# Two layers of a hybrid mixer network on one core: attention stacks fetched a head ahead, two or three merge blocks put ahead of the first scores, and layer 1's middle modulations made in layer 0's ConvFFN

## The chip, the core and the metric

The kernel runs on one core of a Trainium2 chip. The metric is the device time of one execution in microseconds (us). Before the change the median of three runs is 2433.31 us, the lowest 2432.21 and the highest 2433.33. TensorE (PE) multiplies matrices, VectorE (DVE) and ScalarE (ACT) work on tiles in on-chip memory, POOL (GpSimd) here does little but issue transfers, and SP (SyncE) issues the loads of weights. TensorE takes its instructions in the order in which they stand in the program, as each of the engines does.

## What is computed

512 latent tokens and 256 context tokens of width 1024 go through two layers. Each layer normalises the tokens, scales and shifts them with modulations made from a conditioning vector (adaLN), feeds four mixers and their gates from one input projection, merges the four with gates, projects, adds, normalises again, and runs a gated feed-forward network with a short convolution (ConvFFN, 2816 wide). One of the four mixers is differential attention with four heads of two score maps each:

```python
def _diff_softmax(q, k, v, lam):
    s = jnp.einsum('bhcqd,bhckd->bhcqk', q, k).astype(F32) * (DA_HEAD ** -0.5)
    p = jax.nn.softmax(s, axis=-1)
    w = p[:, :, 0] - lam * p[:, :, 1]
    return jnp.einsum('bhqk,bhkv->bhqv', w.astype(v.dtype), v)

def _adaln(cond, w, b, n_chunks):
    m = jax.nn.silu(cond) @ w[:, :n_chunks * D_MODEL] + b[:n_chunks * D_MODEL]
    return [t[:, None, :] for t in jnp.split(m, n_chunks, axis=-1)]
```

Latent tokens read context and latent tokens (768 keys), context tokens read only context (256 keys). In the second layer the context gives only its keys, values and states; its outputs aren't needed, so layer 1 has 512 query tokens and layer 0 has 768. Queries and keys are normalised per head and rotated before the scores.

## The kernel before

Activations lie channel-major: a tile has 128 channels as partitions and up to 768 tokens as columns. All large products are made in high and low parts: `load_split` loads a weight block (`load_raw`, L179, three buffers, SP's queue), casts its high part on ScalarE (L191) and subtracts on VectorE for the low part (L192); `proj` (L204) makes three matmuls for each pair of blocks (L218), 512 or 256 columns wide.

Modulations (`ada`, L258): 24 pairs of blocks for each layer, named by `PAIRS`. A pair is two loads of 512 KB, sixteen small matmuls (L280), a copy and a closing (L267). `FIRST` holds pairs 0 to 7 (shift and scale of the first norm), `REST` pairs 8 to 19 (the gate of the mixers, shift and scale of the second norm), `LAST` pairs 20 to 23 (the gate of the ConvFFN). Layer l's `REST` runs between the blocks of its own merges; `LAST` and the next layer's `FIRST` run in its ConvFFN, one step after each of its 22 blocks.

Attention (`da_mix`, L882): for each pair of heads `da_prep` (L843) normalises and rotates q and k, splits them into high and low parts and spills them to DRAM (`dstk00q` is layer 0, pair 0, q), on POOL's queue (L861). `da_stack` (L865) loads them back for one head, stacked so that high and low parts meet in one product: four loads for q (L874, tile `dstq`) and two for k (L877, tile `dstk`). Both take tiles from a pool with tag z, which has eight buffers; the values `dv` hold two of them for the whole attention. Then, for each block of 128 queries, `scores` makes four matmuls (two for context queries) into one PSUM tile `ps_s` of three banks, of which there is one buffer (L920 to L927), reduces it to the negated maximum on VectorE (`d_nm`, L929) and takes two exponentials on ScalarE (L933). `values` handles two query blocks: it weighs on VectorE (L940 to L943), transposes on TensorE (`ps_wt`, L949), copies to `dwT` (tag h, six buffers) on ScalarE, and multiplies with the values (`ps_o`, L964). It is called three query blocks behind the scores (`DA_AHEAD`). The stack of a head is asked for when the head begins.

Merges: `merge_branch` (L1208) goes over eight blocks of output channels; for each it makes a gate (`gate`, L1203, 24 or 48 matmuls `ps_g`, a tanh), then the product of the branch (`ps_p`), and two VectorE operations. In layer 1 the six gates of the last branch are made early, into buffers of tag h.

The order on the engines is set by a scheduler, which takes instructions by priority and by its estimate of when they are ready: mixers are written with a high priority (`MIXER_FIRST`), so that merge blocks and modulations, written behind the mixer, fill what it leaves on TensorE. `tc.issue_after(x)` holds an instruction back until x stands in the order.

Of the kernel before, what the change touches and what calls it, by code (L numbers as in the profile page):

```python
# [8 lines left out]
F32 = mybir.dt.float32  # L9
# [8 lines left out]
P = 128  # L18
D = 1024
KT = 8  # L20
# [17 lines left out]
DA_AHEAD = 3  # L38
EARLY = 6
# [15 lines left out]
# pairs of ada blocks (chunk * KT + k): shift1 and scale1, gate1, shift2 and scale2, gate2  # L55
# [23 lines left out]
def backbone(ctx, tc, xT, cT, w_ada, w_in, w_v, w_ga, w_branch, w_out, w_up, w_down, vec,  # L79
# [6 lines left out]
    gp_ = ctx.enter_context(tc.tile_pool(name="gp", bufs=25))  # L86
# [10 lines left out]
    def Z(name, shape=None, dt=F32):  # L97
        return gp_.tile(shape or [P, T], dt, tag="z", name=name, bufs=8)
# [57 lines left out]
    # recurrence gates: half biases and LRU_C / 2 times the log-sigmoid of the decay  # L156
# [20 lines left out]
    last = [None]  # L177

    def load_raw(src, nk=KT, cols=P, tag="wraw"):  # L179
        t = wp.tile([P, nk, cols], F32, tag=tag, name="wraw", bufs=3)  # L180
        last[0] = nc.sync.dma_start(t, src).ins
        return t
# [21 lines left out]
    def proj(name, w, act, sg, use, c0=0, cut=None, late=False):  # L204
        """use(ps, a, b) takes the product for the tokens a..b; a cut splits the products, not what use gets;
        late: the low parts of the activations come last"""
        whi, wlo = w
        n = len(act)
        for (a, b) in sg:
            ps = PF(name)  # L210
            step = cut or b - a
            for c in range(a, b, step):
# [4 lines left out]
                for i, (k, wt, x_) in enumerate(terms):  # L217
                    nc.tensor.matmul(ps[:, c - a:d - a], wt[:, k, c0:c0 + P], act[k][x_][:, c:d],  # L218
                                     start=i == 0, stop=i == 3 * n - 1)
            use(ps[:, 0:b - a], a, b)  # L220

    def proj_all(name, loads, act, parts, use, tail=2):
        """the blocks m of a product; use(m, ps, a, b); the last ones go part by part"""
# [10 lines left out]
    def proj_tok(l, which, h, name):  # L234
        """token-major values: tiles of three token blocks"""
# [20 lines left out]
    mods = [cpool.tile([P, 48, 2], F32, name=f"mod{l}") for l in range(DEPTH)]  # L256

    def ada(l, pairs, first=False):  # L258
        """pair p makes the blocks PAIRS[p] of the modulations"""
# [46 lines left out]
    def norm_mod(l, x, g, sh, sc, parts, marks=(None, None)):  # L306
        """the parts are normalised one after the other"""
# [68 lines left out]
    # rstd over partition groups of size n (block-ones matrix bo)  # L376
# [12 lines left out]
    # accurate exp on a small tile  # L389
# [38 lines left out]
    def s5_prep(l):  # L428
# [40 lines left out]
        # unit phasor of 8 steps  # L469
# [5 lines left out]
        # input gains k = (lb - 1) / lam  # L475
# [18 lines left out]
        # phasor tables  # L494
# [25 lines left out]
        for hf in range(2):  # L520
            kps = []
            for d in range(2):
# [16 lines left out]
                # C * lam^k, k = 0..8 (reversed order for the backward direction)  # L539
# [43 lines left out]
                # Bb * lam^k: k = 7 - s (forward), s (backward)  # L583
# [259 lines left out]
    def da_prep(l, i, qk, sg, qgs, rp):  # L843
        """normalised, rotated q and k of heads 2i, 2i+1, parked as exact high and low parts"""
# [38 lines left out]
    def da_mix(l, qks, vt_, lat_only):  # L883
# [25 lines left out]
        stks = [da_prep(l, i, qks[i], sg, qgs, rp) for i in range(2)]  # L909
        o = None  # L910

# [25 lines left out]
        def weights(hd, qt, k0, l2, ps_):  # L937
            """the weights of a head, transposed"""
# [17 lines left out]
        def values(pr):  # L956
            """two blocks of queries of a head, side by side in the array"""
# [22 lines left out]
        for hd in range(4):  # L980
            st = da_stack(stks[hd // 2], hd % 2, sg)
            for qt in range(e // P):
                pend.append(scores(hd, qt, *st))
# [191 lines left out]

    def chain(*gens):
        for g in gens:
            yield from g
# [7 lines left out]
    def weave(main, fill, n=1, flush=True):  # L1186
        """Emit the steps of main with n steps of fill after each of them; returns main's value."""
# [20 lines left out]
    def merge_branch(l, b, h, y, acc, sg, first, gates=()):  # L1208
        """gates: those of the first blocks, where they are there already"""
# [279 lines left out]
```

## Time and profile before

| | us |
|---|---|
| median of three runs | 2433.31 |
| span of the profiled execution | 2429.0 |
| TensorE busy | 2290.4 (94%) |
| VectorE busy | 1322.8 (54%) |
| ScalarE busy | 917.3 (38%) |
| POOL busy | 101.6 (4%) |

The profiled execution lies 4.3 us below the median, which also counts what lies around the span. Below, stretches of the program are named by their time in this span: layer 0's attention stage is 438.8 to 693, its last merges and its ConvFFN 693 to 1446, layer 1's attention stage 1728 to 1967. In a row of a timeline the bracket is the idle time of the engine just before the instruction, and what ended it. PEclk is the granted clock of TensorE as a share of its upper level, 2.4 GHz; 0.50 is the lower level, 1.2 GHz.

### The profile page before, as it was taken

What the parts mean: (1) busy time and instruction counts of PE and PEld (TensorE: products, weight loads), DVE (VectorE), ACT (ScalarE), POOL (GpSimd) and SP (SyncE); (2) the same over time, 40 slices, a digit from 0 to 9 for tenths busy, and PEclk for the clock granted to TensorE, in tenths of its full rate; (3) what the DMA queues carried; (4) which work ended last, traced back from release to release, by engine and by line L of the source; (5) the groups of instructions that cost most, each with busy time, mean ns of one, the idle gap of its engine ahead of it and who ended that gap; (6) DMA issues with size and microseconds to landing.
All of it is one profiled execution on the core that took longest, in us unless ns stands there. A gap on an engine that the chain in (4) does not pass through costs nothing.

```text
span 2429.0 us, 34598 instructions
## 1 busy us (share of the span) xinstructions
PE 2290.4 (94%) x13848; PEld 1906.5 (78%) x13848; DVE 1322.8 (54%) x2831; ACT 917.3 (38%) x1430; POOL 101.6 (4%) x164
## 2 busy tenths in 40 slices
PE   6999999688899999999999999999877899999999
PEld 4788788576788878888888887878655689888887
DVE  7786564565584495343334366557454556444443
ACT  6734134334442243122221247522533454323322
POOL 0010000100000010000000000000110000000000
PEclk9999989889999999999999989999988899999999
DMA  7243243533223233222222232244445324332332
GB/s 259 81 138 121 81 127 107 128 96 87 76 96 117 72 123 122 74 96 63 94 76 81 80 121 72 77 144 156 123 117 127 91 88 130 130 104 87 95 106 86
DMA packets 128176, 258.04 MB, mean 106 GB/s; under 512 B 52816, under 2 KB 61072, under 8 KB 128016
## 3 DMA queue, kind: packets, MB, share of 16 engines
q1 hardware_dynamic: 85136, 222.13, 28.8%
q0 software_dynamic: 42880, 33.70, 5.7%
q8 instruction: 109, 1.79, 0.3%
q14 instruction: 51, 0.42, 0.1%
HBM read 230.78 MB, written 24.87 MB: 105 GB/s over the span
## 4 chain that ended last, share of the span: by engine, by line
PE 67%; issue 22%; DMA 5%; DVE 2%; ACT 2%; POOL 1%; SPq 0%; POOLq 0%; ACTq 0%; DVEq 0%
PE ps_fd L218 13%; PE ps_fa L218 11%; PE ps_fg L218 11%; PE ps_g L218 9%; PE ps_p L218 2%; PE ps_wo L218 2%; PE ps_vdv L244 1%; PE ps_vgv L244 1%; PE ps_u L218 1%; PE ps_lx L218 1%; PE ps_gg L218 1%; PE ps_ada L280 1%; PE ps_ly L218 1%; DMA wraw<-in_w_in_dram 1%; PE ps_go L1138 1%
## 5 line engine op out<-in xcount | busy, mean ns | idle before, releaser
L191 ACT CAST whi<-wraw 128x1024 fp32r<-128x1024 f32 (+2 forms) x284 | 280.6, 989 | 645.0 <-PE ps_fd L218 209.5
L192 DVE TENSOR_TENSOR wlo<-wraw,whi 128x1024 fp32r<-128x1024 f32 (+2 forms) x284 | 325.6, 1147 | 306.5 <-ACT whi L191 282.7
L218 PE MATMUL ps_g<-hi,whi 128*128 128x512 f32 (+1 forms) x768 | 283.7, 369 | 5.2 <-ACT gate L1205 4.5
L218 PE MATMUL ps_g<-lo,whi 128*128 128x512 f32 (+1 forms) x768 | 279.8, 364 | 0.0
L218 PE MATMUL ps_g<-hi,wlo 128*128 128x512 f32 (+1 forms) x768 | 279.6, 364 | 0.0
L218 PE MATMUL ps_fg<-hi,whi 128*128 128x512 f32 (+1 forms) x544 | 194.0, 358 | 3.2 <-ACT hi L364 3.1
L218 PE MATMUL ps_fg<-hi,wlo 128*128 128x512 f32 (+1 forms) x544 | 190.9, 352 | 0.0
L218 PE MATMUL ps_fa<-hi,whi 128*128 128x512 f32 (+1 forms) x528 | 188.1, 356 | 0.0
L218 PE MATMUL ps_fa<-hi,wlo 128*128 128x512 f32 (+1 forms) x528 | 187.3, 355 | 0.0
L218 PE MATMUL ps_fa<-lo,whi 128*128 128x512 f32 (+1 forms) x528 | 187.0, 354 | 0.0
L218 PE MATMUL ps_fd<-ulo,whi 128*128 128x512 f32 (+1 forms) x528 | 186.8, 354 | 0.0
L218 PE MATMUL ps_fd<-uhi,whi 128*128 128x512 f32 (+1 forms) x528 | 186.3, 355 | 0.1
L218 PE MATMUL ps_fg<-lo,whi 128*128 128x512 f32 (+1 forms) x544 | 186.1, 351 | 0.0
L218 PE MATMUL ps_fd<-uhi,wlo 128*128 128x512 f32 (+1 forms) x528 | 186.0, 354 | 0.0
L218 PEld LDWEIGHTS ps_g<-hi,whi 128*128 128x128 f32 x768 | 148.6, 194 | 35.8 <-ACT gate L1205 7.0
L218 PEld LDWEIGHTS ps_g<-hi,wlo 128*128 128x128 f32 x768 | 148.6, 193 | 23.4 <-issue 2.7
L218 PEld LDWEIGHTS ps_g<-lo,whi 128*128 128x128 f32 x768 | 148.7, 194 | 22.7 <-issue 2.7
L1274 DVE SCALAR_TENSOR_TENSOR x<-ps_fd,mod,x 128x512 f32<-128x512 f32 (+1 forms) x96 | 62.9, 660 | 161.6 <-PE ps_fd L218 161.6
L218 PEld LDWEIGHTS ps_fg<-hi,whi 128*128 128x128 f32 x544 | 104.5, 192 | 23.5 <-ACT hi L364 5.3
L929 DVE TENSOR_REDUCE d_nm<-ps_s 128x2 f32<-128x1536 f32 (+1 forms) x40 | 61.6, 1541 | 105.8 <-PE ps_s L923 101.0
L218 PEld LDWEIGHTS ps_fg<-hi,wlo 128*128 128x128 f32 x544 | 104.9, 193 | 13.6
L1267 DVE TENSOR_TENSOR fy<-ps_fa,fy 128x512 f32<-128x512 f32 x66 | 39.8, 602 | 137.7 <-PE ps_fa L218 136.2
(471 smaller groups left out, 4812.7 us busy)
## 6 DMA issues: line engine op xcount, KB each, us to landing
wraw<-in_w_ada_dram SPq DMA_DIRECT2D x96, 512.0 KB, 4.5
wraw<-in_w_in_dram SPq DMA_DIRECT2D x92, 512.0 KB, 3.5
wraw<-in_w_up_dram SPq DMA_DIRECT2D x88, 512.0 KB, 3.4
wraw<-in_w_down_dram SPq DMA_DIRECT2D x32, 384.0 KB, 3.2
wraw<-in_w_down_dram SPq DMA_DIRECT2D x32, 320.0 KB, 3.0
wraw<-in_w_branch_dram SPq DMA_DIRECT2D x16, 512.0 KB, 3.5
wraw<-in_w_out_dram SPq DMA_DIRECT2D x16, 512.0 KB, 3.7
x<-in_xT_dram SPq DMA_DIRECT2D x16, 384.0 KB, 4.4
```

The source lines that it names most:

```text
L191: nc.scalar.copy(hi, raw)
L192: nc.vector.tensor_sub(lo, raw, f32(hi))
L218: nc.tensor.matmul(ps[:, c - a:d - a], wt[:, k, c0:c0 + P], act[k][x_][:, c:d], start=i == 0, stop=i == 3 * n - 1)
L244: nc.tensor.matmul(ps[:, 0:256], a[:, tt * P:(tt + 1) * P], wt[:, k % 4, :], start=st, stop=sp_)
L280: mi = nc.tensor.matmul(ps[32 * g:32 * g + 32, 0:2 * P], cs[:, 4 * j + g, :], raw[:, g, :], start=j == 0, stop=j == 1, tile_position=(0, 3 ...
L929: v.tensor_reduce(nm, sv, AX.X, ALU.max, negate=True)
L1138: nc.tensor.matmul(po[:, oc:oc + 64], sb_[d][:, cc, 2 * pr_:2 * pr_ + 2, :].rearrange("p h v -> p (h v)"), dirs[d][0][:, c * 64:c * 64 + 6 ...
L1267: proj("ps_fa", wa, h, sg, lambda ps, a, b: v.tensor_mul(y[:, a:b], ps, y[:, a:b]), late=f < LATE2)
L1274: v.scalar_tensor_tensor(x[m][:, a:b], ps, mods[l][:, 5 * KT + m, i:i + 1], x[m][:, a:b], op0=ALU.mult, op1=ALU.add)
```

## The change

The stack of head `hd + 1` is asked for when head `hd` begins, and that of head 0 before the second pair of heads is prepared. Tag z has ten buffers instead of eight, so that two stacks fit beside `dv`. The first two steps of `da_mix` are written ahead of the merges; then two (layer 0) or three (layer 1) blocks of branch 3's merge are written, and the first scores are held back until the last matmul of these stands in the order. Layer 1's `REST` moves into layer 0's ConvFFN, behind layer 1's `FIRST`, and each block of a ConvFFN is now followed by two steps instead of one. Raw weights get a fourth buffer. To pay for the buffers, the on-chip area for the descriptors of POOL's transfers falls from its default of 16384 bytes a partition to 4096.

```diff
+DA_LEAD = (2, 3)
...
-    gp_ = ctx.enter_context(tc.tile_pool(name="gp", bufs=25))
+    gp_ = ctx.enter_context(tc.tile_pool(name="gp", bufs=27))
...
     def Z(name, shape=None, dt=F32):
-        return gp_.tile(shape or [P, T], dt, tag="z", name=name, bufs=8)
+        return gp_.tile(shape or [P, T], dt, tag="z", name=name, bufs=10)
...
     def load_raw(src, nk=KT, cols=P, tag="wraw"):
-        t = wp.tile([P, nk, cols], F32, tag=tag, name="wraw", bufs=3)
+        t = wp.tile([P, nk, cols], F32, tag=tag, name="wraw", bufs=4 if tag == "wraw" else 3)
...
-                    nc.tensor.matmul(ps[:, c - a:d - a], wt[:, k, c0:c0 + P], act[k][x_][:, c:d],
-                                     start=i == 0, stop=i == 3 * n - 1)
+                    lastp[0] = nc.tensor.matmul(ps[:, c - a:d - a], wt[:, k, c0:c0 + P], act[k][x_][:, c:d],
+                                                start=i == 0, stop=i == 3 * n - 1).ins
...
-        stks = [da_prep(l, i, qks[i], sg, qgs, rp) for i in range(2)]
+        stks = [da_prep(l, 0, qks[0], sg, qgs, rp)]
+        st = da_stack(stks[0], 0, sg)
+        stks.append(da_prep(l, 1, qks[1], sg, qgs, rp))
         o = None
+        lead = yield
...
         for hd in range(4):
-            st = da_stack(stks[hd // 2], hd % 2, sg)
+            cur = st
+            if hd < 3:
+                st = da_stack(stks[(hd + 1) // 2], (hd + 1) % 2, sg)
             for qt in range(e // P):
-                pend.append(scores(hd, qt, *st))
+                with tc.issue_after(lead) if hd == 0 and qt == 0 else nullcontext():
+                    pend.append(scores(hd, qt, *cur))
...
+    def sent(gen, value):
+        try:
+            gen.send(value)
+            while True:
+                yield
+                next(gen)
+        except StopIteration as s:
+            return s.value
...
-        rest = ada(l, REST)
+        rest = ada(l, REST) if l == 0 else iter(())
         acc = []
-        if l > 0:
-            for _ in range(FILL1):
-                next(rest)
...
-        yd_ = mixer(da_mix(l, (qk0, qk1), dv, lat_only))
-        drain(zipgen(merge_branch(l, 3, h, yg, acc, sg, False), rest, 1))
+        dm = da_mix(l, (qk0, qk1), dv, lat_only)
+        with first():
+            next(dm)
+            next(dm)
+        mb = merge_branch(l, 3, h, yg, acc, sg, False)
+        for _ in range(DA_LEAD[l]):
+            next(mb)
+            next(rest, None)
+        yd_ = mixer(sent(dm, lastp[0]))
+        drain(zipgen(mb, rest, 1))
...
-        nxt = chain(ada(l, LAST), *([ada(l + 1, FIRST)] if l + 1 < DEPTH else []))
+        nxt = chain(ada(l, LAST), *([ada(l + 1, FIRST), ada(l + 1, REST)] if l + 1 < DEPTH else []))
...
-        ffn(l, h, x, sg, lambda: next(nxt, None))
+        def side():
+            for _ in range(2):
+                next(nxt, None)
+        ffn(l, h, x, sg, side)
...
-    nc = _bacc.Bacc("TRN2", target_bir_lowering=False, num_devices=1)
+    nc = _bacc.Bacc("TRN2", target_bir_lowering=False, num_devices=1, dynamic_dma_scratch_size=4096)
```

Three places of the engines' orders follow; the lines of the changed kernel are some two to eight higher for the same statement. First POOL in layer 0's attention, from the k loads of head 0 on, before the change (`dstq<-dstk00q` and `dstk<-dstk00k` load the heads of pair 0, `01` those of pair 1; the rows with `dhi` and `dlo` are the spills of pair 1):

```order
L877 DMA dstk<-dstk00k 128x1x768 x2
L861 DMA dstk01q<-dhi 4x32x768
L861 DMA dstk01q<-dlo 4x32x768
L874 DMA dstq<-dstk00q 64x1x768 x2
L861 DMA dstk01k<-dhi 4x32x768
L861 DMA dstk01k<-dlo 4x32x768
L874 DMA dstq<-dstk00q 64x1x768 x2
L877 DMA dstk<-dstk00k 128x1x768 x2
L874 DMA dstq<-dstk01q 64x1x768 x4
L877 DMA dstk<-dstk01k 128x1x768 x2
```

and after it:

```order
L879 DMA dstk<-dstk00k 128x1x768 x2
L876 DMA dstq<-dstk00q 64x1x768 x4
L863 DMA dstk01q<-dhi 4x32x768
L863 DMA dstk01q<-dlo 4x32x768
L879 DMA dstk<-dstk00k 128x1x768
L863 DMA dstk01k<-dhi 4x32x768
L863 DMA dstk01k<-dlo 4x32x768
L879 DMA dstk<-dstk00k 128x1x768
L876 DMA dstq<-dstk01q 64x1x768 x4
L879 DMA dstk<-dstk01k 128x1x768 x2
```

Head 1's four q loads stood behind both q spills of pair 1 and around its k spills, and now follow head 0's k loads as one piece; its k loads are now on either side of the k spills.

Then TensorE in layer 1 around the first scores of head 0 (L920 to L923 before, L925 to L928 after; `ps_g` and `ps_p` are matmuls of merge blocks, `ps_ada` those of modulations), before the change:

```order
L218 MATMUL ps_p<-ylo,whi 128x512
L218 MATMUL ps_p<-yhi,wlo 128x512
L280 MATMUL ps_ada<-wraw,cs 32x256 x6
L920 MATMUL ps_s<-dstk,dstq 128x512
L921 MATMUL ps_s<-dstk,dstq 128x256
L280 MATMUL ps_ada<-wraw,cs 32x256 x2
L922 MATMUL ps_s<-dstk,dstq 128x256
L923 MATMUL ps_s<-dstk,dstq 128x512
L218 MATMUL ps_g<-hi,whi 128x512
L218 MATMUL ps_g<-lo,whi 128x512
```

and after it:

```order
L220 MATMUL ps_g<-hi,whi 128x512
L220 MATMUL ps_g<-lo,whi 128x512
L220 MATMUL ps_g<-hi,wlo 128x512
L220 MATMUL ps_g<-hi,whi 128x512
L925 MATMUL ps_s<-dstk,dstq 128x512
L926 MATMUL ps_s<-dstk,dstq 128x256
L220 MATMUL ps_g<-lo,whi 128x512
L220 MATMUL ps_g<-hi,wlo 128x512
L220 MATMUL ps_g<-hi,whi 128x512
L927 MATMUL ps_s<-dstk,dstq 128x256
L928 MATMUL ps_s<-dstk,dstq 128x512
L220 MATMUL ps_g<-lo,whi 128x512
```

The pairs of modulations between the scores are gone, and gate matmuls of the third merge block stand there. Between the squares of q (`dqss`) and these scores 96 matmuls of 512 columns of merge blocks stood before, and 132 stand now.

Last, TensorE at the last scores of layer 1's attention (`ps_wt` are the transposes of the weights, `ps_o` the products with the values), before the change:

```order
L218 MATMUL ps_g<-hi,wlo 128x512
L218 MATMUL ps_g<-hi,whi 128x512
L920 MATMUL ps_s<-dstk,dstq 128x512
L921 MATMUL ps_s<-dstk,dstq 128x256
L922 MATMUL ps_s<-dstk,dstq 128x256
L923 MATMUL ps_s<-dstk,dstq 128x512
L964 MATMUL ps_o<-dwT,dv_14997 64x128 x6
L964 MATMUL ps_o<-dwT,dv_14998 64x128 x6
L949 MATMUL ps_wt<-cst,dp 128x128 x4
L218 MATMUL ps_g<-lo,whi 128x512
L218 MATMUL ps_g<-hi,wlo 128x512
```

and after it:

```order
L954 MATMUL ps_wt<-cst,dp 128x128 x6
L925 MATMUL ps_s<-dstk,dstq 128x512
L926 MATMUL ps_s<-dstk,dstq 128x256
L927 MATMUL ps_s<-dstk,dstq 128x256
L928 MATMUL ps_s<-dstk,dstq 128x512
L954 MATMUL ps_wt<-cst,dp 128x128 x6
L925 MATMUL ps_s<-dstk,dstq 128x512
L926 MATMUL ps_s<-dstk,dstq 128x256
L927 MATMUL ps_s<-dstk,dstq 128x256
L928 MATMUL ps_s<-dstk,dstq 128x512
L969 MATMUL ps_o<-dwT,dv_15126 64x128 x6
L969 MATMUL ps_o<-dwT,dv_15127 64x128 x6
```

Before, gate matmuls stand ahead of the last scores and behind the transposes; now, from the fourth query block of head 2 to the end of head 3, only transposes and products with the values stand between the scores, and the gate matmuls follow behind the last of these.

## Rows read from the trace of the kernel before

**Rows 1.** Windows by stage: us, TensorE busy (records), PEclk, DMA share, GB/s
```profile
438.80:693.00 254.20, 206.25 (x1333) 0.89 0.36 94
693.00:1446.00 753.00, 745.12 (x4472) 0.99 0.29 94
...
1728.00:1967.00 239.00, 194.71 (x1027) 0.87 0.44 114
...
sum 2429.00, PE 2290.38; mean PE 381.73
```

**Rows 2.** Timeline of TensorE at each head's first scores: start, us, instruction, idle before
```profile
456.73 0.77 PE L920 MATMUL ps_s<-dstk,dstq 128*128 128x512 f32 x1 [17.88 <-issue]
...
525.11 0.77 PE L920 MATMUL ps_s<-dstk,dstq 128*128 128x512 f32 x1 [7.28 <-DMA dstk<-dstk00k]
...
581.89 0.76 PE L920 MATMUL ps_s<-dstk,dstq 128*128 128x512 f32 x1 [9.54 <-DMA dstk<-dstk01k]
...
637.19 0.76 PE L920 MATMUL ps_s<-dstk,dstq 128*128 128x512 f32 x1 [8.31 <-DMA dstk<-dstk01k]
...
1772.90 0.77 PE L920 MATMUL ps_s<-dstk,dstq 128*128 128x512 f32 x1 [14.93 <-issue]
...
1835.53 0.77 PE L920 MATMUL ps_s<-dstk,dstq 128*128 128x512 f32 x1 [8.87 <-DMA dstk<-dstk10k]
...
1878.63 0.77 PE L920 MATMUL ps_s<-dstk,dstq 128*128 128x512 f32 x1 [6.34 <-DMA dstk<-dstk11k]
...
1922.24 0.76 PE L920 MATMUL ps_s<-dstk,dstq 128*128 128x512 f32 x1 [6.18 <-issue]
```

**Rows 3.** Windows of TensorE behind the six later waits, the last one and the sum
```profile
1918.97:1932.62 13.65, 9.46 (x30) 0.50 0.14 37
sum 61.44, PE 36.19; mean PE 6.03
```

**Rows 4.** Timeline of POOL at requests of head 1, layer 0, and of layer 1
```profile
509.53 1.57 POOL L877 DMA_DIRECT2D dstk<-dstk00k  x2 [36.56 <-PE ps_ada L267]
...
1731.14 0.75 POOL L861 DMA_DIRECT2D dstk10q<-dhi  x1 [25.39 <-ACT dhi L197]
...
1864.17 1.57 POOL L877 DMA_DIRECT2D dstk<-dstk11k  x2 [43.14 <-PE ps_s L923]
```

**Rows 5.** DMA queues and issues from 509 to 526 us: packets, MB, share; KB, us to landing
```profile
q0 software_dynamic: 4192, 1.59, 57.9%
...
dstk<-dstk00k POOLq DMA_DIRECT2D x2, 384.0 KB, 15.2
```

**Rows 6.** Window from the squares of q to layer 1's first scores, columns as in Rows 1
```profile
1723.80:1773.00 49.20, 30.89 (x140) 0.82 0.60 145
```

**Rows 7.** Timeline of TensorE in that window: a modulation pair, first and last of 27 matmuls
```profile
1733.21 1.07 PE L280 MATMUL ps_ada<-wraw,cs 128*32 128x256 f32 x16
...
1736.06 0.39 PE L218 MATMUL ps_g<-hi,wlo 128*128 128x512 f32 x1
...
1741.98 0.39 PE L218 MATMUL ps_p<-ylo,whi 128*128 128x512 f32 x1
```

**Rows 8.** Groups by line and shape, 1770 to 1965: count, busy us, mean ns, idle before
```profile
L933 ACT ACTIVATE dp<-ps_s,d_nm 128x768 f32<-128x768 f32 x32 | 28.6, 901 | 9.6 <-DVE d_nm L929 8.9 <-ACT dwT L951 0.7
L929 DVE TENSOR_REDUCE d_nm<-ps_s 128x2 f32<-128x1536 f32 x16 | 28.1, 1754 | 36.6 <-PE ps_s L923 36.6
...
L949 PE MATMUL ps_wt<-cst,dp 128*128 128x128 f32 x96 | 17.2, 300 | 0.6 <-ACT dwT L951 0.6
L943 DVE SCALAR_TENSOR_TENSOR dp<-dp,d_rl 128x768 f32<-128x768 f32 x16 | 16.3, 1018 | 0.5
...
L964 PE MATMUL ps_o<-dwT,dv 128*64 128x128 f32 x187 | 14.6, 284 | 0.1
```

**Rows 9.** DMA issues of the whole run: count, KB each, median us to landing
```profile
wraw<-in_w_ada_dram SPq DMA_DIRECT2D x96, 512.0 KB, 4.5
...
dstk00k<-dhi POOLq DMA_DIRECT2D x1, 384.0 KB, 8.9
```

More of the change, by code (lines that the diff above doesn't have):

```diff
@@ L177, in backbone @@
     last = [None]
+    lastp = [None]
     def load_raw(src, nk=KT, cols=P, tag="wraw"):
-        t = wp.tile([P, nk, cols], F32, tag=tag, name="wraw", bufs=3)
+        t = wp.tile([P, nk, cols], F32, tag=tag, name="wraw", bufs=4 if tag == "wraw" else 3)
         last[0] = nc.sync.dma_start(t, src).ins
```

## The prediction

> **What bounds the kernel now.** I read the busy time of TensorE stage by stage first [rows 1]. Over the whole it is busy for 2290.38 us of a span of 2429.00, so no other engine can be the bound, and the change can win only time that TensorE does not use. The span lies 4.3 us below the median of the runs, 2433.31; the sum is made on the span and carried over to the median.
>
> From 693 to 1446 us (layer 0's last merges and its ConvFFN) TensorE is idle for 7.9 us in 753. In the two attention stages it is idle for 48.0 us in 254.2 (layer 0) and 44.3 us in 239 (layer 1), and the granted clock averages 0.89 and 0.87 there. These two are the stages to look at.
>
> Next, TensorE's timeline at the first scores of each head (L920); the bracket is the idle time before [rows 2]. Layer 0 waits 17.88 us for head 0, then 7.28, 9.54 and 8.31 for heads 1 to 3. Layer 1 waits 14.93 for head 0, then 8.87, 6.34 and 6.18. Of the six later waits five end with the DMA of a k stack (`dstk`); the sixth is put down to "issue", and stands at the same place of the same loop. The six sum to 25.13 + 21.39 = 46.5 us.
>
> Each wait also takes the clock. In the six stretches right behind them, one of which is shown, the granted clock is 0.50, the lower level (1.2 GHz), and TensorE is busy in them for 36.19 us [rows 3]. At the upper level the same work takes half, so the price is 18.1 us. The six head changes together cost 46.5 + 18.1 = **64.6 us**.
>
> Why a stack is late: POOL's requests stand until TensorE's last work on an earlier head releases buffers. In layer 0 head 1's k stack is asked for at 509.53, after 36.56 us of standing; in layer 1 head 2's at 1864.17, after 43.14 us, released by `ps_s` [rows 4]. The scores of these heads begin 15.6 and 14.5 us later [rows 2]. In the first of these stretches a head's loads put 4192 packets into the software queue, and a k load takes 15.2 us to land [rows 5].
>
> The Trainium skill, page "DMA: Bandwidth & Descriptors", section "Anatomy of one DMA — SWDGE (gpsimd) path", gives a fit of 2.0 us plus bytes over 436e3 per us, which makes an estimate of 2.9 us for such a load. The rows say 15.2, and the measurement decides. By the page the loads would have some 3 us to hide at a head change, and the gain would be nearer 15 than 65.
>
> **The change part by part.** *Stacks a head ahead.* With ten tiles instead of eight the next head's loads are asked for while the present head runs. In POOL's order head 1's four q loads now follow head 0's k loads directly, and head 2's loads wait for head 0's last scores, not head 1's. From one head's first scores to the next are 43 to 68 us [rows 2], and a stack takes about 15 [rows 5]: it lands at least 25 us before it is wanted, and all six waits go, 64.6 us. What is late next is the softmax chain of the head itself. As a lower bound some waits shrink to 2 or 3 us and keep a piece of their low clock: 50 us.
>
> *Merge blocks ahead of the first scores.* In layer 0 TensorE's order up to the first scores is the same before and after, so the 17.88 us stay. In layer 1 the way from the squares of q (1723.8) to the first scores takes 49.2 us, of which TensorE is busy for 30.89 [rows 6]; about 2.6 of these are lost to a low clock (0.82 on average), so there are 28.2 us of work and 21 lost. The way is one of spills and loads, on POOL from 1731.14 on [rows 4], and stays as it is. After the change 132 matmuls of 512 columns stand on it. From 1736.06 to 1741.98 26 such follow each other [rows 7], 0.228 us each: 30.1 us, and 2.2 us of small ones, 32.3. Lost: 49.2 - 32.3 = 16.9 instead of 21, a gain of **4 us** (0 if the way grows, 9 if it shortens).
>
> *What these blocks no longer cover.* They are missing at the end of layer 1's attention. Before, up to 19 gate matmuls stand between the last blocks of scores; after, from the fourth query block of head 2 on, five blocks of scores follow with nothing between but transposes and values. The gates that could stand there come after the last transposes: their buffers (tag h) are those of the transposed weights. So the time there is that of the chain. There is one score buffer, and each block of scores waits for the reduction of the block before, 1.754 us, and its two exponentials of 0.901 [rows 8]; with about 1 us of matmuls, the reads of the sums and the hops that is 5.2 us. Five blocks are 26 us. VectorE's weighing of a pair (L943, 1.018 each, and smaller ones) pushes in ahead of a reduction twice, some 4 us, and the last pair's weighing, transposes, copies and values add 5: 35 us in all. TensorE's work in it is 38 transposes (96 take 17.2 us, so 6.8), 48 value products (187 take 14.6, so 3.7) [rows 8] and 4 us of scores, 14.5 us. Lost: 20.5 us, and up to 7 us more where the chain's matmuls run at the low clock that stands behind waits of this kind [rows 3]. I take **-24 us**. The ends are 15 (the steps of the chain overlap better than one after the other) and 32 (low clock throughout and 5 us behind it).
>
> *Twelve pairs of modulations moved.* The products of a pair take 1.07 us on TensorE [rows 7], with the closing under 1.6, so under 19 us in all. They leave layer 1 (what filled its first hole is counted in the 28.2) and go to a ConvFFN where TensorE is full already [rows 1]: 0, for work that is moved costs the same in either place. Their 24 loads of 512 KB move along SP's queue into that ConvFFN, with a fourth buffer for raw weights. A load lands in 4.5 us [rows 9]; if each pair showed one landing, that would be 12 x 4.5 = 54 us. Twelve pairs run among the blocks of that ConvFFN already, in a stage with 7.9 us of idle time in all [rows 1], so I keep 0, and -5 as the end.
>
> *The rest.* The mixer's first two steps go out earlier, and the descriptor area of POOL's transfers falls from 16384 to 4096 bytes: 0 each by the rows, the second with a rival of its own (below). Smaller waits in layer 1's attention may go or move: 5 us either way.
>
> **Sum:** 64.6 + 4 - 24 = 44.6 us; 2433.3 - 44.6 = 2388.7, say **2388 us**. The ends give 64.6 + 9 - 15 + 5 = 64 us and 50 + 0 - 32 - 10 = 8 us of gain, so 2369 to 2425.
>
> **The rivals.** (1) *The tail is cheap.* ScalarE and VectorE have few weight splits left there, pairs overlap, and the tail costs 8 us, the first hole gains 9: 64.6 + 9 - 8 = 66, **2368 us**. Against it: there is one score buffer.
>
> (2) *Layer 1 gives nothing.* The waits go, but without work to hide it the chain shows in head 2 as well: the tail costs 37 us, and 64.6 - 37 = 28 is left, **2405 us**. For it: the first blocks are used up before head 0, so the work that is left is thinner everywhere behind.
>
> (3) *The stacks still come late.* POOL asks in the order written, and a head's loads may stand behind spills or buffers, so that one layer keeps its three waits (about 32 us): 64.6 - 32 - 24 = 9, **2424 us**. Against it: the loads wait for scores a whole head earlier.
>
> (4) *Slower.* The smaller descriptor area makes POOL's transfers go one after the other. The first head's chain in layer 1 is ten transfers in 41.8 us (1731.14 to 1772.90 [rows 2, 4]), since they overlap in pairs. One by one, with 8.9 us for a spill of 384 KB [rows 9] and about 4 for a q load, six and four of them take 69 us, 27 more; in both layers 54, at the place where TensorE has no work left: 2388 + 54 = **2442 us**. It decides from 22 us a layer on (half of 44.6). For it: a head's loads are 4192 packets [rows 5], 262 for each of 16 DMA engines. Against it: the transfers of a chain wait for each other in pairs anyway.
>
> By the Trainium skill, same page, sections "Terms" and "SWDGE vs HWDGE vs iDMA", a descriptor has 16 bytes and POOL writes them into rings in SBUF; as an estimate 4096 bytes hold 256 for one DMA engine, fewer than the 262. By that rule POOL would stand within every set of loads, if only for the last few. No row shows it.
>
> **How the numbers follow.** The forecast (2379 to 2399) has 0.50, rival 1 0.18, rival 2 0.18, rivals 3 and 4 0.07 each. The range that leaves about 2 in 10 out takes in most of rivals 1 and 2: 2366 to 2412. About 0.2% (5 us) is what a measurement of this kernel can tell from no change. Faster: 0.50 + 0.18 + 0.18 and the better part of rival 3, 0.90; same, its worse part and the edge of rival 4, 0.04; slower, 0.06.
>
> **What would show it.** After the change the first scores of heads 1 to 3 should have no idle time over 2 us before them and the clock at 1.00, with k loads issued 25 us or more ahead. Before head 0's scores about 18 us should stand in layer 0, and 12 to 17 in layer 1. In the last 35 us of layer 1's attention TensorE should be at 40% and wait for the reduction and the exponentials. Layer 0's ConvFFN should be longer by up to 19 us, as full as before. I am wrong if work covers the tail, if the loads of a stack wait on POOL, or if loads of modulations show as waits in the ConvFFN.

## The result, and the profile after

The changed kernel takes 2371.41 us (median of four runs, 2370.35 to 2374.39) against 2432.76 of the kernel before beside it: a ratio of 0.9753 on record, with a 95% interval of 0.9733 to 0.9773 (the two medians alone give 0.9748). The forecast was 2388 with a range of 2366 to 2412. The time lies inside the range, but below the 2379 to 2399 that stood for the forecast itself. The sign, the places and the largest term were right; the gain was 61 us where the sum gave 44.6.

The profiled execution has a span of 2368.6 us, 60.4 less than that of before. TensorE is busy for 2262.0 us of it (96%). To see where the 60.4 us lie, both traces are cut at the same points of the program. The windows of TensorE after the change, with the columns of [rows 1]:

```profile
0.00:436.47 436.47, 404.35 (x2858) 0.97 0.41 132
436.47:819.00 382.53, 355.22 (x2254) 0.96 0.37 104
819.00:1433.90 614.90, 607.64 (x3776) 0.99 0.34 109
1433.90:1762.60 328.70, 313.80 (x2012) 0.98 0.35 101
1762.60:1995.60 233.00, 212.93 (x1280) 0.95 0.37 101
1995.60:2368.60 373.00, 368.09 (x1672) 0.99 0.32 99
```

The same cuts in the trace of before, from the same view:

| stage | before, us | after, us | difference |
|---|---|---|---|
| up to the wait before layer 0's first scores | 438.85 | 436.47 | -2.4 |
| from there to layer 0's ConvFFN | 414.25 | 382.53 | -31.7 |
| layer 0's ConvFFN | 595.8 | 614.9 | +19.1 |
| layer 1 up to its first scores | 324.1 | 328.7 | +4.6 |
| from there to layer 1's ConvFFN | 282.6 | 233.0 | -49.6 |
| layer 1's ConvFFN | 373.4 | 373.0 | -0.4 |

The timeline of TensorE at the first scores of the heads, the rows that answer to [rows 2] (L925 is L920 of before):

```profile
457.46 0.77 PE L925 MATMUL ps_s<-dstk,dstq 128*128 128x512 f32 x1 [20.99 <-DMA dstq<-dstk00q]
...
511.19 0.39 PE L925 MATMUL ps_s<-dstk,dstq 128*128 128x512 f32 x1
...
554.41 0.50 PE L925 MATMUL ps_s<-dstk,dstq 128*128 128x512 f32 x1
...
597.63 0.50 PE L925 MATMUL ps_s<-dstk,dstq 128*128 128x512 f32 x1
...
1762.58 0.77 PE L925 MATMUL ps_s<-dstk,dstq 128*128 128x512 f32 x1 [14.05 <-DMA dstq<-dstk10q]
...
1807.01 0.39 PE L925 MATMUL ps_s<-dstk,dstq 128*128 128x512 f32 x1
...
1841.69 0.40 PE L925 MATMUL ps_s<-dstk,dstq 128*128 128x512 f32 x1
...
1873.61 0.50 PE L925 MATMUL ps_s<-dstk,dstq 128*128 128x512 f32 x1 [1.72 <-ACT dp L938]
```

Five of the six waits of 6 to 10 us have no bracket any more, and the sixth is 1.72 us and ends with an exponential, not with a stack. The two waits before head 0 stand, 20.99 and 14.05 us. From one head's first scores to the next layer 0 now takes 43 to 54 us, where it took 55 to 68. Before the first scores of heads 1 to 3, in both layers, the clock is not lowered either: PEclk is 1.00 from 462.6 to 660.4 and from 1766.5 to 1875.6 us.

The second k load of a head, the last of its six loads, is now issued 27 to 39 us before the head's first scores, where it was 12 to 18 us. POOL's timeline has it for head 1 of either layer (columns as in [rows 4]; the scores begin at 511.19 and 1807.01):

```profile
472.21 0.83 POOL L879 DMA_DIRECT2D dstk<-dstk00k  x1
...
1779.98 0.82 POOL L879 DMA_DIRECT2D dstk<-dstk10k  x1
```

The end of layer 1's attention, TensorE's timeline from the fourth query block of head 2 on; only instructions with idle time before them are left in, and the last value product:

```profile
1868.18 0.44 PE L954 MATMUL ps_wt<-cst,dp 128*128 128x128 f32 x2 [0.56 <-ACT dwT L956]
...
1871.46 0.44 PE L954 MATMUL ps_wt<-cst,dp 128*128 128x128 f32 x2 [0.68 <-ACT dwT L956]
1873.61 0.50 PE L925 MATMUL ps_s<-dstk,dstq 128*128 128x512 f32 x1 [1.72 <-ACT dp L938]
...
1877.46 1.51 PE L954 MATMUL ps_wt<-cst,dp 128*128 128x128 f32 x6 [2.87 <-ACT dp L938]
...
1884.01 0.50 PE L925 MATMUL ps_s<-dstk,dstq 128*128 128x512 f32 x1 [0.62 <-ACT dp L938]
...
1887.84 0.85 PE L954 MATMUL ps_wt<-cst,dp 128*128 128x128 f32 x6 [2.65 <-ACT dp L938]
...
1897.27 1.51 PE L954 MATMUL ps_wt<-cst,dp 128*128 128x128 f32 x6 [3.53 <-DVE dp L948]
1899.09 2.83 PE L969 MATMUL ps_o<-dwT,dv 128*64 128x128 f32 x24 [0.30 <-ACT dwT L956]
```

Here are the waits for the exponentials and the weighing that were expected. They lie from 1866.7 to 1901.9, 35.2 us long.

### The profile page after: what moved, and what is told of

It is laid out like the page before. It is cut to its first block, busy times and chain, and to the rows that moved or that the text cites. A ratio compares the mean times of both kernels' runs of the same rounds, so it can differ in the third digit from the quotient of the medians.

```text
span 2368.6 us, 34594 instructions
## 1 busy us (share of the span) xinstructions
PE 2262.0 (96%) x13848; PEld 1895.3 (80%) x13848; DVE 1327.7 (56%) x2831; ACT 914.5 (39%) x1428; POOL 101.3 (4%) x164
## 5 line engine op out<-in xcount | busy, mean ns | idle before, releaser
L220 PE MATMUL ps_g<-hi,whi 128*128 128x512 f32 (+1 forms) x768 | 278.8, 363 | 2.8 <-DVE gate L1242 2.8
L220 PEld LDWEIGHTS ps_fg<-hi,whi 128*128 128x128 f32 x544 | 104.5, 192 | 31.5 <-ACT hi L366 8.9
L220 PEld LDWEIGHTS ps_fd<-uhi,whi 128*128 128x128 f32 x528 | 99.8, 189 | 15.7 <-DVE fy L1285 1.6
```

The costliest lines, as they stand in the source:

```text
L220: lastp[0] = nc.tensor.matmul(ps[:, c - a:d - a], wt[:, k, c0:c0 + P], act[k][x_][:, c:d], start=i == 0, stop=i == 3 * n - 1).ins
```

## The experiments

The theory at the start: the gain is the six waits, which go because the next head's stack is asked for a head earlier, less a tail in layer 1 that has lost its cover; the moved modulations are neutral. The rivals: the smaller descriptor area costs something, the place of the requests in the code is what counts, or other parts of the change carry the gain. Each ratio below is the one on record, to runs of the kernel before on the same chip; it differs from the quotient of the medians by up to 0.0011, which is 3 us, so differences of a few us between these kernels are not to be trusted.

**The descriptor area alone.** The kernel before with one edit:

```diff
-    nc = _bacc.Bacc("TRN2", target_bir_lowering=False, num_devices=1)
+    nc = _bacc.Bacc("TRN2", target_bir_lowering=False, num_devices=1, dynamic_dma_scratch_size=4096)
```

> The kernel before with one change: the descriptor area of POOL's transfers is 4096 bytes instead of 16384. My theory: POOL stands some 10 us inside a set of six loads (in the changed kernel it stood 10.21 us at 457.68 and 12.43 at 1750.69 with nothing else to wait for), but where it stands it holds up only the loads of the next head or the last of a set, so the time stays within 6 us of 2433 (2430 to 2439), with the k loads of heads 1 to 3 landing at most 2 us later. The rival, the smaller area puts transfers one after the other in the first head's chain: both first waits grow by 15 us or more, 2463 or above.

Measured: 2428.62 us, ratio 0.9987 (0.9972 to 1.0003), no difference. POOL does stand, as its timeline shows; columns as in [rows 4]:

```profile
512.15 1.57 POOL L877 DMA_DIRECT2D dstk<-dstk00k  x2 [37.64 <-PE ps_ada L267]
513.69 1.99 POOL L874 DMA_DIRECT2D dstq<-dstk01q  x3
528.44 0.65 POOL L874 DMA_DIRECT2D dstq<-dstk01q  x1 [12.77 <-issue]
```

Two k loads and three q loads go out at once, the fourth q load 12.77 us later, at the time when the set's k loads have landed (15.7 us from issue to landing). What is late is a load for the head after the one that is waited for, so nobody misses it. With the area of 16384 bytes four such loads go out in one piece, in 2.63 us, at the same place of the trace of before (511.07). Rival 4 of the forecast saw a real standstill and gave it a price that it doesn't have. Of the two standstills that were named ahead of this run one was misread: the 12.43 us at 1750.69 in the changed kernel stand where this run has 12.99 us that end with the landing of a k spill. The standstill of that set is the next one, 8.10 us at 1762.80.

**The ten buffers alone.** The kernel before with

```diff
-        return gp_.tile(shape or [P, T], dt, tag="z", name=name, bufs=8)
+        return gp_.tile(shape or [P, T], dt, tag="z", name=name, bufs=10)
```

and the two sizes that go with it (pool and descriptor area). The call of `da_stack` stays where a head begins.

> The kernel before with ten buffers of tag z instead of eight and the area of 4096 bytes that pays for them; stacks are still asked for in the code when a head begins, no merge block is written ahead, and layer 1's modulations stay in layer 1. Theory: the buffers alone let the scheduler's order ask for the stacks a head ahead, so the six waits go (64.6 us), and since the modulations still fill the end of layer 1's attention the tail stays small: 2433 - 65 + 4 to 10 for the tail, 2367 to 2380. Rival 1: the place of the call is what counts, the waits stay, 2425 to 2437. Rival 2: the moved modulations bring 10 us or more of the gain (4 before the first scores, the rest since their work costs less in the ConvFFN), so this kernel is slower than the changed one, 2381 to 2395.

Measured: 2381.55 us, ratio 0.9796 (0.9763 to 0.9829). The six waits are gone here too; TensorE's timeline at heads 1 to 3 of layer 0:

```profile
515.54 0.39 PE L920 MATMUL ps_s<-dstk,dstq 128*128 128x512 f32 x1
...
559.67 0.40 PE L920 MATMUL ps_s<-dstk,dstq 128*128 128x512 f32 x1
...
602.14 0.40 PE L920 MATMUL ps_s<-dstk,dstq 128*128 128x512 f32 x1
```

POOL's order of spills and loads is, load for load, that of the changed kernel. So it is the buffers that let the loads go early, and the scheduler finds the place itself; the call a head ahead adds nothing to that order. In layer 1 none of these waits is left either. The time came out just above the range of the theory, in that of the second rival, but four runs scatter from 2376 to 2391 us and don't separate the two: with its wide interval this kernel has 42 to 58 of the 61 us.

**Eight buffers in the changed kernel**, all the rest of the change in place (the same line, back to `bufs=8`).

> The changed kernel with eight buffers of tag z as before; all the rest of the change stays. Theory: the six waits of 6 to 10 us come back with their low clock, and the end of layer 1's attention, which is without work to fill it, stays as it is: 2371 + 55 to 65, 2426 to 2436, so all of the gain is lost. Rival: the early requests and moved modulations bring a third of the gain by themselves, 2405 to 2418.

Measured: 2424.3 us, ratio 0.9963 (0.9951 to 0.9976). All six waits are back, 6.62 to 10.66 us each; three of them:

```profile
517.61 0.76 PE L925 MATMUL ps_s<-dstk,dstq 128*128 128x512 f32 x1 [6.62 <-DMA dstq<-dstk01q]
...
576.10 0.77 PE L925 MATMUL ps_s<-dstk,dstq 128*128 128x512 f32 x1 [10.66 <-DMA dstk<-dstk01k]
...
1886.77 0.77 PE L925 MATMUL ps_s<-dstk,dstq 128*128 128x512 f32 x1 [6.71 <-DMA dstk<-dstk11k]
```

Taking the buffers away costs 51 us of the gain by the ratios (0.9963 against 0.9753), putting them in alone brings 50. The two agree, and leave some 10 us for everything else in the change together (6 to 12 by the interval of this run). None of the single edits below accounts for them clear of the noise.

**No merge block ahead of the first scores.**

```diff
-DA_LEAD = (2, 3)
+DA_LEAD = (0, 0)
```

> The changed kernel with no merge block written ahead of the first scores (0 in both layers instead of 2 and 3). TensorE's, VectorE's, ScalarE's and SP's orders come out the same as with the blocks; only some POOL instructions stand elsewhere. Theory: the scheduler puts those blocks there anyway, so no difference, 2371 within 4 us, with a first wait of layer 1 of 12 to 16 us as before. Rival: the hold on the first scores matters by itself, 5 us or more either way.

Measured: 2372.1 us, ratio 0.9747 (0.9724 to 0.9771), the same as the changed kernel, with a wait of 14.00 us before layer 1's first scores. TensorE's order is the same, instruction for instruction, with none as with two and three blocks: the scheduler puts that work there anyway. What put more of it ahead of layer 1's first scores is that the modulations, which stood between, went away: with them back, in the next run, the 132 matmuls of 512 columns on that way fall to 112.

**Modulations back in layer 1.**

```diff
-        rest = ada(l, REST) if l == 0 else iter(())
+        rest = ada(l, REST)
...
-        nxt = chain(ada(l, LAST), *([ada(l + 1, FIRST), ada(l + 1, REST)] if l + 1 < DEPTH else []))
+        nxt = chain(ada(l, LAST), *([ada(l + 1, FIRST)] if l + 1 < DEPTH else []))
```

> The changed kernel with layer 1's twelve pairs of modulations back between layer 1's merge blocks. By the traces so far layer 1 then loses 45 us instead of 46 and a pair's work costs 4 us more in all, so theory 1: 2371 + 4 to 8, 2374 to 2380. Theory 2, the move is worth what is left of the whole gain beside the buffers (61 - 51 = 10 us): 2380 to 2384. Rival, the move is worth nothing and the rest came from the fourth raw buffer: 2369 to 2373.

Measured: 2373.83 us, ratio 0.9767 (0.9749 to 0.9785). That is 2 to 3 us slower than the changed kernel, which the intervals don't separate from nothing. The trace shows what was traded: the first wait is 16.86 us instead of 14.05, and no wait at the end of the attention is over 1.2 us. Counting as lost the idle time and half of the busy time at the lower clock, layer 1 up to its ConvFFN loses 41.9 us against 46.2 in the changed kernel. Its work at full clock is 24.2 us more, of which layer 0's ConvFFN saves 19.8. The two nearly cancel: the move is worth next to nothing, and its tail of 20 us (see below) is not its net price. With the ten buffers alone, where nothing is moved, layer 1 loses 46.7 us as well.

```profile
1745.67 0.77 PE L925 MATMUL ps_s<-dstk,dstq 128*128 128x512 f32 x1 [16.86 <-issue]
```

**Three buffers for raw weights.**

```diff
-        t = wp.tile([P, nk, cols], F32, tag=tag, name="wraw", bufs=4 if tag == "wraw" else 3)
+        t = wp.tile([P, nk, cols], F32, tag=tag, name="wraw", bufs=3)
```

> The changed kernel with three buffers for raw weights as before, instead of four. The kernel with the buffers of tag z alone came out at a ratio of 0.9796, the one with all but the moved modulations at 0.9767, the changed one at 0.9753. If the step from the first to the second is the fourth raw buffer: 7 us slower than the changed kernel, 2375 to 2381, with more waits of TensorE for weights. Rival, the step is scatter between runs and the buffer does nothing: 2369 to 2374.

Measured: 2379.57 us, ratio 0.9757 (0.9742 to 0.9773), on a chip where the kernel before took 2436.08. By the ratio the buffer is worth nothing that can be told, by the medians 5 us; in the trace three waits come back, 4.22, 2.18 and 2.11 us. The first stands at the same scores in every kernel with three buffers (3.28 us before, 4.91 in the first run, 3.37 in the second), as does the last (2.15, 3.03 and 2.06); the changed kernel and the third and fourth runs, with four, have neither. So the fourth buffer removes these waits; what that is worth in time stays open.

```profile
493.12 0.79 PE L925 MATMUL ps_s<-dstk,dstq 128*128 128x512 f32 x1 [4.22 <-ACT dp L938]
...
1440.76 0.79 PE L220 MATMUL ps_lx<-hi,whi 128*128 128x512 f32 x1 [2.11 <-ACT hi L366]
...
1462.41 2.39 PE L804 MATMUL ps_ri<-xc,lruw 128*128 128x512 f32 x4 [2.18 <-DVE xc L776]
```

The other runs ask whether the two waits that are left, and the tail, can be had.

**Six blocks ahead in layer 0** (`DA_LEAD = (6, 3)`; here TensorE's order does change, 224 more matmuls stand ahead of the first scores).

> The changed kernel with six merge blocks of branch 3 ahead of layer 0's first scores instead of two (layer 1 as it was). In TensorE's order three more blocks, some 31 us of work, now stand ahead of these scores than in the changed kernel; two and none gave the same order. Theory: the first wait of layer 0 (20.99 us in the changed kernel, with about 4 us of low clock behind it) is a chain of transfers that this work covers, and there is enough other work behind, so 2371 - 18 to 25: 2346 to 2353, with under 3 us of idle time before the first scores. Rival: the work is only moved and is missing at the end of layer 0's attention, 2365 to 2372.

Measured: 2366.54 us, ratio 0.9719 (0.9692 to 0.9745), about 5 to 8 us better than the changed kernel where 18 to 25 were expected; the two intervals overlap. The wait before the first scores is gone but for 3.59 us at its start, and others have come at the end of the same attention:

```profile
440.30 1.07 PE L282 MATMUL ps_ada<-wraw,cs 128*32 128x256 f32 x16 [3.59 <-ACT gate L1223]
...
663.42 2.93 PE L254 MATMUL doss<-dosq,cst 128*128 128x512 f32 x4 [1.80 <-ACT dosq L382]
...
670.98 1.43 PE L220 MATMUL ps_p<-yhi,whi 128*128 128x512 f32 x3 [3.73 <-ACT yhi L199]
```

The same 45.6 us from the wait on hold 39.33 us of TensorE's work, instead of 23.88. But the last merge (`ps_p` from `yhi`) now waits for the attention's own output, whose last norm has no work to cover it: from 640 us to the output projection the stage has 6.5 us of idle time, 3.4 more than the changed kernel has from 640 on, and it runs at a clock of 0.95 against 0.98. The theory was right that the work covers the wait, but the time is in the rival's range: the work that is put ahead is missing behind.

**Early gates in other buffers.**

```diff
-        early = [gate(l, 2, m, h, sg, H("gate")) for m in range(EARLY if lat_only else 0)]
+        early = [gate(l, 2, m, h, sg, (Z if m < 4 else H)("gate", [P, 512])) for m in range(EARLY if lat_only else 0)]
```

> The changed kernel with four of the six early gates of layer 1 put into buffers of tag z, which the stack of head 2 leaves free, instead of tag h. Theory: the end of layer 1's attention (20 us lost in the changed kernel: 13 idle and 7 by the clock) is empty because the gates wait for the buffers of the transposed weights; with gates between the last scores 10 to 16 us come back, 2355 to 2361, with at most 6 us of idle time between head 2's last scores and the last values. Rival: the chain of the softmax sets the end whatever stands between, and the gates only move, 2367 to 2373.

Measured: 2368.38 us, ratio 0.9727 (0.9703 to 0.9752), 3 to 6 us better instead of 10 to 16, with intervals that overlap, and so in the rival's range. The gates do move between the last scores, and the waits there go, but the last query blocks and the attention's output stand bare instead:

```profile
1901.39 0.50 PE L925 MATMUL ps_s<-dstk,dstq 128*128 128x512 f32 x1 [1.44 <-ACT dp L938]
...
1905.22 1.32 PE L954 MATMUL ps_wt<-cst,dp 128*128 128x128 f32 x6 [2.87 <-DVE dp L948]
1908.18 1.51 PE L954 MATMUL ps_wt<-cst,dp 128*128 128x128 f32 x6 [1.64 <-DVE dp L948]
...
1919.30 1.22 PE L220 MATMUL ps_p<-yhi,whi 128*128 128x512 f32 x2 [4.24 <-ACT yhi L199]
```

**Both**, and then both with the modulations back in layer 1 and eight blocks ahead there (`DA_LEAD = (6, 8)`).

> Both edits: six blocks ahead in layer 0, and four early gates in buffers of tag z. Theory: they lie in different layers and add up, 2371 - 28 to 41: 2330 to 2343. Rival: if either is only moved work, no better than the better one alone, 2346 or more.

> As with both edits, but layer 1's twelve pairs of modulations stay in layer 1 and eight merge blocks stand ahead of its first scores, so that the first wait of layer 1 (14 us) is covered with merge blocks and the tail with modulations and gates. Theory: the lost time of layer 1 falls by a further 10 to 15 us against the kernel with both edits, less 4 us since a pair takes longer there than in the ConvFFN: 2322 to 2337. Rival: moving the pairs into the ConvFFN is worth 10 us by itself, as the second kernel of the first set against the changed one suggests, and this kernel is 0 to 10 us slower than the one with both edits.

Measured: 2367.93 us, ratio 0.9722 (0.9696 to 0.9747), and 2367.92 us, 0.9722 (0.9691 to 0.9753). Neither adds anything to the better of the single edits, and the theories' 2343 and 2337 us at most were missed by 25 and 31 us. In the last one the wait before layer 1's first scores is covered, and 5.68, 4.16 and 5.27 us stand at the end of the attention and behind it instead.

**Transfers by SP instead of POOL**, first spills and loads (the k loads by the same edit as the q loads, which are shown), then the loads alone with the spills on ScalarE's queue.

```diff
-                nc.gpsimd.dma_start(dd[:, p_, :, :n], f32(t_[:, :n]))
+                nc.sync.dma_start(dd[:, p_, :, :n], f32(t_[:, :n]))
...
-                        nc.gpsimd.dma_start(t[64 * p_:64 * p_ + 64, :n],
+                        nc.sync.dma_start(f32(t[64 * p_:64 * p_ + 64, :n]),
```

> The changed kernel with the spills and the stack loads issued by SP instead of POOL (no software queue). The first waits, 20.99 us in layer 0 and 14.05 in layer 1, are chains of four steps of software transfers of 8 to 15 us each; SP's weight loads of 512 KB land in 3.5 to 5 us. Theory 1: the software queue is what takes the time, each step falls to 4 to 6 us, and the two first waits shrink to under 5 us together: 2336 to 2350. Theory 2: the small pieces (rows of some 380 bytes on average) take the time on any queue, steps stay at 8 us or more and the gain is under 8 us: 2363 to 2373. Rival: SP stands until a spill or a buffer is ready, with the weight loads behind it, and TensorE waits for weights: 2380 or more.

> As the kernel with SP's transfers, but the spills are issued by ScalarE's queue and only the loads by SP. If the queue is what counts: 2336 to 2350 as well. If SP's standing is what hurts in the other, this one is better by 5 us or more; if ScalarE's standing for the low parts hurts its casts, worse by as much.

Measured: 2455.31 us, ratio 1.0097 (1.0078 to 1.0117), and 2453.45 us, 1.0089 (1.0073 to 1.0106): some 1% slower than before. The first waits grow to 27.65 and 19.37 us in the first of the two. SP's timeline there shows why the weights suffer too (a row runs from the start of its first issue to the end of its last):

```profile
423.81 4.83 SPq L876 DMA_DIRECT2D dstq<-dstk00q  x4
...
453.86 17.76 SPq L876 DMA_DIRECT2D dstq<-dstk00q  x4
471.66 4.05 SPq L863 DMA_DIRECT2D dstk01q<-dhi  x1
475.75 4.61 SPq L183 DMA_DIRECT2D wraw<-in_w_ada_dram  x2
```

The first four q loads took SP 0.48 to 0.53 us each, with 2.70 us of waiting between the second and the third, no more than POOL, which issued two of them in 1.35 us. The next four, behind two k loads, took 0.62, 9.15, 3.89 and 3.96 us: SP is held by the issues themselves, and spills and weights stand behind them. A weight load at 505.22 held it for 7.33 us. ScalarE then waits 10.87 us for a weight load (to 525.70), and TensorE 9.62 us for a gate behind it (to 527.08). Where the spills are issued makes no difference. Both theories of the first of these runs missed; its rival (2380 or more, with weights behind transfers on SP) had the outcome, but from 453.86 on it is the issues that hold SP, not only waits until a spill or a buffer is ready.

## Why the prediction was right, and where it was off

**The six waits, 64.6 us: right in size.** All six are gone. In layer 0 the stage is 31.7 us shorter, with the first wait 3.1 us longer and a small wait of 3.28 us gone with it; 25.13 of idle time and half of the low-clock work there make 33 of the 64.6, so that 31.5 of 33 came. In layer 1 the idle time of its three waits fell from 21.39 to 1.72 us. The reason given was also right, the buffers, but the step that told of "requests a head ahead" as an edit of the code was not needed: the second run shows that two more buffers do it alone, and the third that all the rest does not do it without them.

**Layer 0's first wait: right that it stays, off by 3 us.** It grew from 17.88 to 20.99. Head 1's q loads now follow head 0's k loads at once, in the same queue, and the row says `DMA dstq<-dstk00q`. POOL's timeline has the standstill of the smaller area at this place too, with the rest of the set going out after the first scores:

```profile
445.48 1.98 POOL L876 DMA_DIRECT2D dstq<-dstk00q  x3
457.68 0.66 POOL L876 DMA_DIRECT2D dstq<-dstk00q  x1 [10.21 <-issue]
```

The wait goes with the buffers: in the three kernels with eight and POOL's queue it is 17.60 to 18.52 us, the first run's smaller area included, and with ten buffers 19.89 us alone and 20.67 to 22.07 in the others that have no more blocks ahead. That the q loads of head 1 lengthen it by sharing the queue fits this, but was not tried by itself.

**Layer 1's first wait, 4 us: 3 us too small, within its ends of 0 and 9, and the cause wrong.** The wait lost 6.9 us (14.05 against 14.93 + 1.80 + 1.58 and 2.6 of low clock). The step put it down to the merge blocks that the code writes ahead. With none of them written ahead the wait is 14.00; with the modulations back and the blocks written ahead it is 16.86. It was the modulations' leaving that pulled the blocks forward.

**The tail, -24 us: right in shape, 4 us too dear.** It is 35.2 us long, where the chain gave 35. One reading in it was off: 96 products with the values lie in it, not 48, so TensorE's work there is 15.8 us at full clock instead of 14.5, and it is busy for 64% of the stretch, not 40%. The brackets above sum to 12.9 us, and the clock costs more, as the window says (columns of [rows 1]):

```profile
1866.00:1902.00 36.00, 22.88 (x163) 0.78 0.05 15
```

Of its busy time from 1866 to 1903 us TensorE has 13.8 us at the lower clock, half of which, 6.9, is the price: 20 us lost in all. The forecast had the idle time and the clock together at 20.5 to 27.5.

**The moved modulations, 0: off by about 4 us.** The ConvFFN of layer 0 is 19.1 us longer, as the sum of under 19 said. But TensorE's work in layer 1 up to its ConvFFN, counted at full clock (busy time less half of what lies in stretches at the lower clock), fell from 538.0 to 515.5 us, by 22.5, where that of the ConvFFN rose by 18.6, counted the same way. The same instructions cost less in the ConvFFN than between the merges (the run with them back has 24.2 and 19.8); why was not tried.

**The rest, "5 us either way": gave 4 us.** In layer 1's attention the small waits of 2.96 us and below and the low clock behind them lost some 9 us before and 4 after, and the stretch before it 2 less; the norm before the ConvFFN lost 3 more (a wait of 4.24 us before the first `ps_fg`). With 2.4 us at the start of the program, 2.9 of the first wait, 4 of the tail and 4 of the modulations, less 1.5 us in layer 0's attention, this makes up the distance between 44.6 and 60.4. The 2.4 us are scatter: in the run without blocks ahead, with the same order on TensorE, the start takes 438.2 us. No single step of the sum failed; that the small terms fell on the same side, and carried the time below the forecast's own 2379 to 2399, no step had foreseen, and the range held because it was drawn wide enough for the rivals.

**The rivals.** Rival 1 (2368 us) came closest to the time, but not by its mechanism: the tail was not cheap. Rival 2 had it at 37 us with the chain showing in head 2 as well; it took 20, from the end of head 2 on. Rival 4's standstill was there and cost nothing that shows in the time. Rival 3's time is that of the third run, but there the waits stand in both layers, and for want of buffers.

By the Trainium skill, page "DMA: Bandwidth & Descriptors", sections "Terms" and "SWDGE vs HWDGE vs iDMA", the area of 4096 bytes should hold, as an estimate, 256 descriptors of 16 bytes for one DMA engine. The trace of the first run agrees with the estimate to the load: two k and three q loads put 229 packets on each engine (3664 in the queue from 512.15 to 528.44) and go out at once, the fourth q load would make 262, and POOL waits 12.77 us with it.

## What to carry to other kernels

A wait at a loop's boundary for a load whose buffers are held by the previous pass is a matter of buffers first: here, where a scheduler sets the order, two more of them brought some 50 of 61 us, and writing the request earlier left the order of the loads as it was. Work that is put in front of one wait is taken from behind it: here 17 us of a covered wait came out as 5 to 8 at most, since the attention's own output then had no cover, so before moving filler ask what stands bare at the end of the same stage. And undo each part of a change by itself, since a part that reads as the cause (blocks written ahead) may leave the engines' order as it was.

## What the runs showed of the hardware that was not expected

Transfers of many small pieces hold the engine that issues them when enough of them are on the way, on either path. At 423.81, with no k load ahead of them, q loads of 192 KB took SP 0.48 to 0.53 us each; behind two k loads the first took 0.62 and the next three 9.15, 3.89 and 3.96 us, and everything that SP had to issue stood behind. POOL spent 2.63 us on four such loads as long as its area had room; with the area of 4096 bytes a load that it no longer held stood 2.3 to 15.4 us. A standstill shows on POOL as an idle bracket with "issue" as its releaser, and on SP as a long duration of the issue itself. Neither sign is proof: the 12.43 us above carry "issue" and fit a wait for a spill, and a merged row of SP can hold waits, as the 4.83 us at 423.81 do.
